# Memory values by tokens, norm weights on ScalarE, four late visits in pairs, and a shorter Newton step in a one-core decoder step

## The chip, the cores and the metric

The kernel runs on one core of a Trainium2 chip. The metric is the device time of one execution in microseconds; the comparison is between medians of several executions. A profile of one execution gives a span, from the first to the last instruction, and the rows that are quoted here.

## What is computed

One layer of a decoder for 256 prompt tokens and 8 samples of 4 new tokens each (288 columns in all), width 2048, in fp32. Cut to what matters here:

```
mkv  = (rms_norm(mem_prompt, mem_norm_g) @ w_mem_kv)     # 256 memory tokens, 4 heads of 128 keys, 4 of 128 values
h    = rms_norm(x, norm_g)
conv, q, kv6, m_q, gates = split(h @ w_in)                # 52 blocks of 128 columns
o_nsa = gated sum of attention to compressed, selected and window keys (paged cache of 2048 past tokens)
o_m   = softmax(m_q mk^T * scale) mv                      # memory attention, no mask
y     = rms_norm(x + concat(conv, silu*o_nsa, silu*o_m) @ w_out, final_g)
```

Outputs are y, the new keys and values, the window buffers, the convolution state and `mkv`.

## The kernel before

Every large product is split for accuracy: weights and activations each into a high part and a remainder, both in a reduced fp32 format (fp32r), and three products (high by high, high by low, low by high) are summed in PSUM. Weights come in halves of 128x1024 (eight 128x128 blocks). For each half `w_load` (line 221) fetches it, `w_hi` (228) makes the high part on ScalarE, `w_lo` (233) the remainder on VectorE, and `product_half` (250) runs 24 matmuls with the weight blocks as the stationary operand and the activations (256 or 288 columns) as the moving one. Half s asks ScalarE for the high part of half s+2 and VectorE for the remainder of half s+1 before its own matmuls, so the remainder of a half is made one half ahead of its use. In matmul 21 of a half the load of half s+6 is issued and one piece of x is fetched (`x_next`, 266).

Order of the program: the memory projection (eight blocks of columns, 16 halves: four blocks of keys, four of values, lines 1358 to 1361), then x's projections (queries, memory queries, keys and values, convolution, gates), then the output projection in two passes and the final norm. The memory projection gives its result as 128 features by 256 tokens. For the values, `mem_tile` (1016) multiplies each block by the tokens' norm factors (`rstd_m`) on VectorE out of PSUM into `mvt`, and `mem_rstd` (878) writes it to memory, transposes it by TensorE in pairs of 128x128 (`mvtp`) and copies it to the planes 12 to 15 of `mixed`, which hold values by tokens for the prompt's memory attention. During the same halves `prep_x` (930) makes x ready: per piece of three planes of 128x288, three VectorE operations that multiply by the norm weight of the plane and by the tokens' factors, then x's high part on ScalarE and the remainder on VectorE.

Everything that is not a large product is written as generators that are resumed at each half of a weight half (`chunk`, 161). A clock of the planner, `at`, adds up assumed costs of what was written and decides when a generator goes on; so the instruction order on each engine is fixed when the program is built, and depends on those costs.

The sampled tokens' attention is staged: tiles of 128x1024 (512 KB) of cached keys, values and windows pass through six buffers `st` (`NST`, 53) and one more that is freed when the prompt's memory queries have been used. `stages` (717) is the list of visits, sorted by a due time; `stage_stream` (746) lets a visit go ahead when its due time, its tiles and the planner's estimate of their landing allow it, `used_up` (742) gives its buffers back and `load_next` (731) issues the next loads, on SP for all but the selected values, which GpSimd gathers by page table (584). A visit is 32 or so small matmuls (fp32, 32 output rows): scores of a page group (`selk_use`, `wink_use`; tile `sk`), memory scores and values (`memk_use`, `memv_use`; `smd`, `omd`), values (`selv_use`, `winv_use`; `od`). Before its values a visit transposes the weights of the next one (`weights`, 556; tile `pv`).

The end: for the last 512 columns of y, tokens lie on partitions. `decode_rows` (1544) sums the samples' part in PSUM tile `zd`, `squares` (1551) adds the residual on VectorE and squares on ScalarE with a sum, `factors` calls `rsqrt` (199), which takes a square root on ScalarE and refines its reciprocal by one Newton step on VectorE.

## Time and profile before

| what | value |
|---|---|
| runs shown | 611.5, 613.99, 619.14 us; median 613.99 |
| the profiled execution | 616.16 us |
| its span | 614.4 us, 13419 instructions |
| mean granted TensorE clock | 0.996 |
| transfers | 190.85 MB, mean 311 GB/s |
| VectorE, ScalarE, GpSimd busy | 461.0, 285.3, 200.5 us |

How to read the rows of the profile. A row of the timeline has the start and the length in us, the engine, the line of the kernel (L120 is the helper that records every matmul, L137 the one for VectorE and ScalarE), the operation, `out<-in` by tile names, the shape, and how many were merged; in brackets stands idle time just before and what ended it. PE is TensorE's matmuls, PEld its weight loads, DVE VectorE, ACT ScalarE, POOL GpSimd, SP the queue that issues most loads. [...] An fp32 matmul leaves two records. A row of the windows view has a stretch, its length, the busy time and count of PE, PEld, DVE, ACT and POOL, the granted clock, the DMA share and GB/s.

### The profile page before, as it was taken

The page shows a single profiled execution, that of the slowest core. Times are in us where ns is not written, and L with a number is a line of the kernel's source. Part 1 is how long each engine was busy: PE and PEld are TensorE (multiplying, and loading weights), DVE is VectorE, ACT ScalarE, POOL GpSimd, SP SyncE. Part 2 cuts the span into 40 slices and gives each one's busy share as a digit, 9 for nine tenths or more (in the row PEclk, how much of TensorE's full clock was granted, in tenths as well). Part 3 has the DMA queues.
Part 4 walks back from the last instruction along what each step waited for, and adds up shares of the span by engine and source line. Part 5 has one row for each costly group of instructions (what it writes and reads, how often), then busy time and mean ns, then how long its engine had stood idle before and what let it go on. Part 6 is the DMA issues. An engine that isn't in the chain of part 4 may idle for free.

```text
span 614.4 us, 13419 instructions
## 1 busy us (share of the span) xinstructions
PE 603.0 (98%) x4919; PEld 554.0 (90%) x4919; DVE 461.0 (75%) x749; ACT 285.3 (46%) x499; POOL 200.5 (33%) x282
## 2 busy tenths in 40 slices
PE   8999999999999999999999999999999999999997
PEld 5999999989799999989889889899889989889995
DVE  4879899988485779989789888897668733357666
ACT  4755445543355444435334434543543544335552
POOL 2012544533124442433453552323111336222200
PEclk8999999999999999999999999999999999999999
DMA  8999798999968999798878898999899998859834
GB/s 285 394 403 404 258 320 300 345 310 337 365 203 280 370 407 375 250 387 298 310 232 313 284 386 273 309 318 311 289 334 332 336 353 291 288 195 411 281 130 155
DMA packets 76226, 190.85 MB, mean 311 GB/s; under 512 B 8896, under 2 KB 26464, under 8 KB 75904
## 3 DMA queue, kind: packets, MB, share of 16 engines
q0 software_dynamic: 26048, 100.48, 46.0%
q1 hardware_dynamic: 49104, 88.25, 40.4%
q10 hardware_dynamic: 1008, 1.25, 0.6%
q8 instruction: 39, 0.64, 0.4%
q14 instruction: 27, 0.22, 0.1%
HBM read 184.74 MB, written 13.60 MB: 323 GB/s over the span
## 4 chain that ended last, share of the span: by engine, by line
PE 78%; DMA 11%; DVE 8%; issue 2%; SPq 1%; ACT 0%; ACTq 0%; DVEq 0%
PE z L120 56%; DMA st<-ckc 5%; PE zr L120 4%; PE od L120 3%; DMA st<-ckk 3%; PE sk L120 3%; PE zf L120 2%; DVE wl L137 2%; DVE pooled L137 2%; PE acc L120 2%; PE s L120 2%; DMA rx<-xT 1%; DVE st L137 1%; PE pt L125 1%; DMA mraw<-memT 1%
## 5 line engine op out<-in xcount | busy, mean ns | idle before, releaser
L120 PE MATMUL z<-x,wh 128*128 128x288 f32 x1664 | 254.4, 302 | 0.0
L137 DVE TENSOR_TENSOR wl<-w,wh 128x1024 fp32r<-128x1024 f32 x147 | 185.7, 1265 | 84.6 <-PE z L120 34.9
L120 PEld LDWEIGHTS z<-x,wh 128*128 128x128 f32 x1664 | 229.7, 188 | 7.8 <-issue 6.1
L137 ACT ACTIVATE wh<-w 128x1024 fp32r<-128x1024 f32 x148 | 154.3, 1052 | 25.1 <-PE z L120 15.4
L120 PE MATMUL z<-x,wl 128*128 128x288 f32 x832 | 127.2, 295 | 0.3 <-DVE wl L137 0.3
L120 PEld LDWEIGHTS z<-x,wl 128*128 128x128 f32 x832 | 115.7, 188 | 0.8 <-DVE wl L137 0.7
L356 POOL TENSOR_TENSOR st<-st,cst 128x512 f32<-128x512 f32 x63 | 69.3, 1102 | 133.8 <-DVE st L137 49.3
L225 POOL DMA_DIRECT2D w<-w_in x104 | 58.2, 560 | 109.1 <-DVE wl L137 82.4
L137 DVE TENSOR_REDUCE pooled<-st 128x16 f32<-128x1024 f32 x63 | 76.2, 1210 | 5.8 <-POOL st L356 5.8
L137 DVE TENSOR_TENSOR st<-st,cst 128x512 f32<-128x512 f32 x63 | 43.3, 688 | 10.9 <-DMA st<-ckc 10.8
L225 POOL DMA_DIRECT2D w<-w_out x32 | 17.5, 550 | 63.0 <-DVE wl L137 43.1
L584 POOL DMA_INDIRECT st<-ckv,rows_v x26 | 27.1, 1042 | 31.9 <-PE od L120 17.4
L137 ACT ACTIVATE P<-P,nm 128x128 f32<-128x128 f32 (+1 forms) x32 | 14.2, 445 | 29.3 <-DVE nm L137 29.3
L120 PE MATMUL z<-m,wh 128*128 128x256 f32 x192 | 27.3, 287 | 0.5 <-DVE mvt L137 0.5
L120 PE MATMUL z<-y,wh 128*128 128x288 f32 x192 | 27.6, 297 | 0.0
L120 PE MATMUL z<-y1a,wh 128*128 128x288 f32 x168 | 26.7, 299 | 0.0
L120 PEld LDWEIGHTS z<-y,wh 128*128 128x128 f32 x192 | 26.3, 188 | 0.1
L120 PEld LDWEIGHTS z<-y1a,wh 128*128 128x128 f32 x168 | 23.6, 188 | 2.1 <-issue 1.2
L120 PEld LDWEIGHTS z<-m,wh 128*128 128x128 f32 x192 | 24.7, 191 | 0.8 <-issue 0.7
L120 PE MATMUL sk<-st,qz 128*32 128x256 f32 x272 | 20.4, 383 | 1.4 <-DMA st<-ckk 1.2
L120 PE MATMUL od<-st,S 128*32 128x256 f32 x256 | 18.7, 382 | 0.0
L120 PE MATMUL zf<-mixed,w 128*128 128x256 f32 x64 | 16.6, 421 | 1.9 <-DVE mixed L137 1.7
(318 smaller groups left out, 716.2 us busy)
## 6 DMA issues: line engine op xcount, KB each, us to landing
w<-w_in POOLq DMA_DIRECT2D x104, 512.0 KB
st<-ckc SPq DMA_DIRECT2D x126, 256.0 KB, 5.8
w<-w_out POOLq DMA_DIRECT2D x32, 512.0 KB
st<-ckk SPq DMA_DIRECT2D x112, 128.0 KB, 5.1
w<-w_mem SPq DMA_DIRECT2D x12, 512.0 KB, 7.1
o_wk<-wk POOLq DMA_DIRECT2D x8, 512.0 KB
o_wv<-wv POOLq DMA_DIRECT2D x8, 512.0 KB
st<-mv SPq DMA_DIRECT2D x7, 512.0 KB, 7.9
```

Source lines behind the costliest of these rows:

```text
L120: nc.tensor.matmul(out, a, b, **kw)
L125: nc.tensor.transpose(out, a, b)
L137: return getattr(self.engine, name)(*args, **kw)
L225: (nc.gpsimd if s >= ON_SYNC else nc.sync).dma_start(raws[s], wsrc[s])
L356: done.append(eng.tensor_tensor(tm[:, :, kv], tm[:, :, kv], acmp[:, kv].unsqueeze(1).unsqueeze(1).to_broadcast([128, 2, 4, 64]), op=ALU.mu ...
L584: nc.gpsimd.indirect_dma_start(t, None, ckv, bass.IndirectOffsetOnAxis(ap=rows_v[:, j * 4 + b:j * 4 + b + 1], axis=0))
```

## The change

Five edits.

1. The memory values are computed with tokens on the rows: `mem_values` replaces four calls of the block product. The stationary operand is now the split memory activations (128 tokens), the moving one the split weights, 512 columns at once; per half 12 matmuls instead of 24. The host lays these weights out accordingly (`_kpairs`). The norm factor is then one number per partition (`mr`), which ScalarE applies as it copies each of two PSUM tiles `zv` to `mixed`; the transposes and `mvt` go. The output of values is written in two pieces of 256 KB instead of four of 128 KB.
2. x's planes are multiplied by the norm weights on ScalarE as soon as they are loaded (`x_scales`, one piece per half from half 7 on); `prep_x` then multiplies a piece by the tokens' factors in one VectorE operation.
3. Four late visits are held back and run right before the next one: keys 7 with the second window's keys, memory values 0 with 1, selected values 4 with 5 and 6 with 7. For values the weights of both are transposed first. For the buffers that this takes, two more parts of the prompt's key tile `qk1` are freed once the prompt and the first group of samples are done; the samples' new keys, which lie there, are copied aside (`kn`).
4. In the final norms the Newton step has three VectorE operations after the scaled sum instead of four.
5. The samples' residual of the last columns is added by an identity matmul into `zd`, so `squares` and the final gain read PSUM directly.

```diff
+        if rest is not None:
+            act.activation(r, ssq, AF.Sqrt, scale=1.0 / D, bias=rest[0])
+            vec.scalar_tensor_tensor(v, ssq, -0.5 / D, rest[1], op0=ALU.mult, op1=ALU.add)
+            vec.reciprocal(r, r)
+            vec.scalar_tensor_tensor(t, r, r, v, op0=ALU.mult, op1=ALU.mult)
+            vec.scalar_tensor_tensor(r, t, 1.5, r, op0=ALU.add, op1=ALU.mult)
+            return
...
+    def run_half(s, mm, last, between=None):
+        m = len(mm) // 2
+        for n, (out, a, b, start, stop) in enumerate(mm):
...
+            if n == LOAD_AT * m // 12:
+                w_load(s + WR + 1)
+                next(x_next, None)
+                if s > 5:
+                    next(x_scale, None)
+            matmul(out, a, b, start=start, stop=stop)
...
+    def mem_values():
+        z = [pz.tile([128, 512], F32, name=f"zv{tt}", tag="z") for tt in range(2)]
+        def out(tt):
+            planes = mixed[:, 12 + 2 * tt:14 + 2 * tt, 0:256]
+            act.activation(planes, z[tt].rearrange("p (a n) -> p a n", a=2), AF.Copy, scale=mr[:, tt:tt + 1])
+            nc.gpsimd.dma_start(o_memv[tt].rearrange("p (a n) -> p a n", a=2), planes)
+        for h in range(8):
+            s = nhalf[0]
+            nhalf[0] += 1
+            w_hi(s + 2)
+            w_lo(s + 1)
+            wh, wl = his.pop(s), los.pop(s)
+            mm = []
+            for tt in range(2):
+                for k in range(2):
+                    hi, lo = (m_hl[n][:, 2 * h + k, tt * 128:(tt + 1) * 128] for n in range(2))
+                    w = slice(k * 512, (k + 1) * 512)
+                    early = 2 * tt + (k if h == 7 and tt else 0)
+                    mm += [(early, tt, hi, wh[:, w]), (early, tt, lo, wh[:, w]), (2.5 if h == 7 and not tt else 4, tt, hi, wl[:, w])]
+            mm.sort(key=lambda x: x[0])
...
-        if i < 4:
+        if i < 4 and ("PT", hf, i + 1) not in env:
             weights(hf, i + 1)
...
+    HELD = ((selk_use, 7), (memv_use, 0), (selv_use, 4), (selv_use, 6))
...
-            yield from u(j, tiles_of.pop((u, j)))
+            if (u, j) in HELD:
+                held.append((u, j))
+                continue
+            if u is selv_use and held:
+                for q in (j % 4 + 1, j % 4 + 2):
+                    if q < 5 and ("PT", j // 4, q) not in env:
+                        weights(j // 4, q)
+            for u, j in (*held, (u, j)) if u is not cmp_use else ((u, j),):
+                yield from u(j, tiles_of.pop((u, j)))
+                if u is not cmp_use:
+                    used_up(u, j)
...
+    def x_scales():
+        for i in range(6):
+            yield
+            k, t = xg[i]
+            for j in range(t.shape[1] // NT):
+                act.activation(xr[k + j], xr[k + j], AF.Copy, scale=C("ng")[:, k + j:k + j + 1])
...
-                for j in range(k, k + n):
-                    vec.scalar_tensor_tensor(xr[j], xr[j], g[:, j:j + 1], r, op0=ALU.mult, op1=ALU.mult)
+                xv = x.rearrange("p (k n) -> p k n", n=NT)
+                vec.tensor_tensor(xv, xv, r.unsqueeze(1).to_broadcast([128, n, NT]), op=ALU.mult)
...
+        while not env.get(("decoded", 0)):
+            yield 1
+        vec.tensor_copy(kn[1], kk[:, :, 256:NT])
+        for o in (0, 2176):
+            free.append(qk1[:, o:o + 1024])
+            load_next()
...
-    def squares(g, z):
-        vec.tensor_tensor(part[g], z, part[g], op=ALU.add)
-        act.activation(scratch[:, :part[g].shape[1]], part[g], AF.Square, accum_out=sums2[:, g:g + 1])
+    def squares(g):
+        if g < 2:
+            vec.tensor_tensor(part[g], z[g], part[g], op=ALU.add)
+        act.activation(scratch[:, :part[g].shape[1]], y_of[g], AF.Square, accum_out=sums2[:, g:g + 1])
...
+    matmul(zd[:, :128], ident, part[2], start=True, stop=False, skip_group_check=True)
     decode_rows(0, SPREAD_AT)
```

How the edits move instructions, at three places. On ScalarE in the value halves before (`wh` is a weight half's high part, `x_112` x's high part, `rx` a piece of x, `mvtp` transposed values):

```order
L137 ACTIVATE wh_558<-w_411 128x1024
L137 ACTIVATE x_112<-rx 128x864
L137 ACTIVATE wh_603<-w_455 128x1024
L137 ACTIVATE mixed<-mvtp_619 128x128 x2
L137 ACTIVATE x_112<-rx_413 128x864
L137 ACTIVATE wh_651<-w_504 128x1024
```

and now:

```order
L137 ACTIVATE rx<-rx,cst 128x288 x3
L137 ACTIVATE wh_526<-w_411 128x1024
L137 ACTIVATE x_112<-rx 128x864
L137 ACTIVATE rx_413<-rx_413,cst 128x288 x3
L137 ACTIVATE wh_557<-w_448 128x1024
L137 ACTIVATE x_112<-rx_413 128x864
```

Three scalings of 128x288 stand ahead of each weight half's high part, and a piece of x now goes from ScalarE to VectorE and back.

On VectorE in the same halves before (`wl` is a weight half's remainder, `x_113` x's remainder):

```order
L137 SCALAR_TENSOR_TENSOR rx<-rx,cst,rstd_x 128x288 x3
L137 TENSOR_TENSOR x_113<-rx,x_112 128x864
L137 TENSOR_TENSOR wl_605<-w_411,wh_558 128x1024
L137 SCALAR_TENSOR_TENSOR rx_413<-rx_413,cst,rstd_x 128x288 x3
L137 TENSOR_TENSOR mvt<-z_513,Vc 128x256
```

and now:

```order
L137 TENSOR_TENSOR rx<-rx,rstd_x 128x864
L137 TENSOR_TENSOR x_113<-rx,x_112 128x864
L137 TENSOR_TENSOR wl_559<-w_411,wh_526 128x1024
L137 TENSOR_TENSOR rx_413<-rx_413,rstd_x 128x864
L137 TENSOR_TENSOR x_113<-rx,x_112 128x864
```

One operation of 864 columns stands for three of 288, and the value tile's scaling (`mvt`) is gone.

On GpSimd's queue, near the last visits, before (gathers of selected values into `st` and `qk`, weight loads `w`):

```order
L584 DMA st_108<-ckv,rows_v 128x1024
L584 DMA st_104<-ckv,rows_v 128x1024
L584 DMA qk_793<-ckv,rows_v 128x1024
L584 DMA st_105<-ckv,rows_v 128x1024
L225 DMA w_6658<-w_out 128x1024
L225 DMA w_6690<-w_out 128x1024
L225 DMA w_6722<-w_out 128x1024
L584 DMA st_107<-ckv,rows_v 128x1024
```

and now:

```order
L629 DMA qk_665<-ckv,rows_v 128x1024
L629 DMA st_105<-ckv,rows_v 128x1024
L629 DMA st_106<-ckv,rows_v 128x1024
L629 DMA st_107<-ckv,rows_v 128x1024
L629 DMA qk_665<-ckv,rows_v 128x1024 x2
L629 DMA st_108<-ckv,rows_v 128x1024
L229 DMA w_6540<-w_out 128x1024
```

Seven gathers stand in a row where four stood, and the weight loads come behind all of them.

More of the change, by code (lines that the diff above doesn't have):

```diff
@@ L260, in product_half @@
         mm.sort(key=lambda x: x[0])
-        for n, (_, a, b) in enumerate(mm):
+        run_half(s, [(out, a, b, first and n == 0, last and n == 23) for n, (_, a, b) in enumerate(mm)], last)
+    def run_half(s, mm, last, between=None):
+        m = len(mm) // 2
+        for n, (out, a, b, start, stop) in enumerate(mm):
             if s == DIRECT and n == 0:
                 w_load(s + WR)
-            if n == LOAD_AT:
+            if n == LOAD_AT * m // 12:
                 w_load(s + WR + 1)
                 next(x_next, None)
-            matmul(out, a, b, start=(first and n == 0), stop=(last and n == 23))
-            if n == 23 and LOW_FIRST <= s < NH - 18:
+                if s > 5:
+                    next(x_scale, None)
+            matmul(out, a, b, start=start, stop=stop)
+            if n == 2 * m - 1 and LOW_FIRST <= s < NH - 18:
                 w_lo(s + 2)
-            if n % 12 == 11 and not (last and n == 23):
+            if n == 7 and between:
+                between()
+            if n == m - 1:
+                chunk()
+            if n == 2 * m - 1 and not last:
                 chunk()
@@ L305, in first_tiles @@
                     yield z[i]
+    def mem_values():
[18 more added lines that the diff above has]
+            mm.sort(key=lambda x: x[0])
+            i = [[n for n, x in enumerate(mm) if x[1] == tt] for tt in range(2)]
+            run_half(s, [(z[tt], a, b, h == 0 and n == i[tt][0], h == 7 and n == i[tt][-1]) for n, (_, tt, a, b) in enumerate(mm)],
+                     h == 7, (lambda: out(0)) if h == 7 else None)
+        assert "rstd_m" in env
+        out(1)
+        chunk()
     def proj(hi, lo, N):
@@ L771, in decode_step @@
     rstd_m = Vc
+    mr = one.tile([128, 2], F32, name="mr")
     rstd_x = zt("C", "rstd_x")
@@ L917, in token_rstd @@
         yield lag
-        r = small(3, "yr")
         w = len(groups)
@@ L930, in prep_x @@
     def prep_x():
-        g, r = C("ng"), rstd_x
+        r = rstd_x
         flat = lambda t, k, n: t[:, k:k + n, :].rearrange("p k n -> p (k n)")
@@ L1016, in mem_tile @@
     def mem_tile(i, z):
-        dst = mkT[:, i, :] if i < 4 else zt("A", "mvt")[:, :256]
-        if i < 4:
-            act.activation(dst, z, AF.Copy)
-        else:
-            yield 2
-            assert "rstd_m" in env
-            vec.tensor_tensor(dst, z, rstd_m, op=ALU.mult)
-        mem_raw[i] = dst
+        act.activation(mkT[:, i, :], z, AF.Copy)
+        mem_raw[i] = mkT[:, i, :]
+        return
+        yield
     cos, sin = C("cos"), C("sin")
@@ L1359, in decode_step @@
         then(mem_tile(i, z))
-    for i in range(2, 8):
+    for i in range(2, 4):
         then(mem_tile(i, proj(*m_hl, 256)))
+    mem_values()
     qq = xhl.tile([128, 16, 256], F32, name="qq", tag="qk0")
@@ L1530, in decode_step @@
     out = (yo[:, 0:2048], yo[:, 2048:4096], yod)
-    rest, sums2 = small(3, "yrest", 1), small(3, "ysums", 1)
+    rest, sums2 = small(6, "yrest", 1), small(3, "ysums", 1)
     quarters = small(32, "imp", 1)
@@ L1600, in decode_step @@
     rows(z[0], ws[2], 6, y, 0, False, True)
-    vec.tensor_scalar(rest, ssq[:, 0:3], 1.0 / D, EPS, op0=ALU.mult, op1=ALU.add)
-    squares(0, z[0])
+    vec.tensor_scalar(rest[:, 0:3], ssq[:, 0:3], 1.0 / D, EPS, op0=ALU.mult, op1=ALU.add)
+    vec.tensor_scalar(rest[:, 3:6], ssq[:, 0:3], -0.5 / D, -0.5 * EPS, op0=ALU.mult, op1=ALU.add)
+    squares(0)
     gains(0)
```

56 lines of the change are left out of this document (24 added, 32 removed).

## The prediction

> **What bounds the kernel now.** I read the page first: the share of each engine, and the chain that ended last.
>
> ```profile
> PE 603.0 (98%) x4919; PEld 554.0 (90%) x4919; DVE 461.0 (75%) x749; ACT 285.3 (46%) x499; POOL 200.5 (33%) x282
> PE 78%; DMA 11%; DVE 8%; issue 2%; SPq 1%; ACT 0%; ACTq 0%; DVEq 0%
> ```
>
> TensorE fills 603.0 of 614.4 us. So what the change is worth is, to first order, how much it takes out of TensorE's stream and how many waits it puts in. A mean over the span hides who paces whom, so I asked for the busy time by stage: the value projection of the memory tokens, the stretch behind it, and the late stretch in which the last visits lie.
>
> ```profile
> 35.87:60.70 24.83, 24.33 (x201) 24.03 (x200) 23.17 (x37) 14.12 (x20) 6.73 (x12) 1.00 1.03 402
> 60.70:130.00 69.30, 69.01 (x534) 67.59 (x534) 64.22 (x100) 35.45 (x62) 34.62 (x43) 1.00 0.90 305
> 310.00:541.00 231.00, 231.00 (x1985) 207.23 (x1985) 161.66 (x264) 99.33 (x185) 80.30 (x104) 1.00 0.89 311
> ```
>
> The columns are: stretch, length, busy us of PE, PEld, DVE, ACT and POOL, granted clock, DMA share, GB/s. In the first stretch VectorE is busy for 23.17 of 24.83 us, next to TensorE. From 310 to 541 us TensorE has no idle time at all and VectorE has three tenths of its time free. The first stretch is therefore paced by two engines, the last by one.
>
> **Value projection.** Before, eight halves of weights take 24 products of 256 columns each. The cost of one is its step.
>
> ```profile
> 24.15 0.28 PE L120 MATMUL z<-m,wl 128*128 128x256 f32 x1
> 24.27 0.28 PE L120 MATMUL z<-m,wh 128*128 128x256 f32 x1
> 47.91 1.60 PE L120 MATMUL z<-m,wh 128*128 128x256 f32 x12
> 49.35 0.38 PE L125 MATMUL mvtp<-cst,mvt 128*128 128x128 f32 x2
> 49.48 0.72 PE L120 MATMUL z<-m,wh 128*128 128x256 f32 x4
> 50.05 1.12 PE L120 MATMUL z<-m,wl 128*128 128x256 f32 x8
> 592.62 1.09 PE L120 MATMUL zr<-wh,y 128*128 128x512 f32 x4
> 594.01 1.09 PE L120 MATMUL zr<-wh,y 128*128 128x512 f32 x4
> ```
>
> The step at 256 columns is 0.12 us. Products of 512 columns exist in the output stage: six of them (four, and two between the quoted rows) go from 592.62 to 594.01, 0.232 us each. The new form has 96 such products for 192 old ones: 96 x 0.232 = 22.3 us for 192 x 0.12 = 23.0, 0.8 us less. The transposes of the value tiles go too: 16 products and one pair of them take 50.05 - 47.91 = 2.14 us where 16 x 0.12 is 1.92, so a pair costs 0.22. Two pairs lie in this stretch (0.45) and two behind it (0.45). The rest of the 24.83 us is 0.36 for the spread of the norm factors, which stays, and some 1.0 of waits: 24.83 - 23.04 - 0.45 - 0.36.
>
> Those waits are VectorE's.
>
> ```profile
> 49.34 1.37 DVE L137 SCALAR_TENSOR_TENSOR rx<-rx,cst,rstd_x 128x288 f32<-128x288 f32 x3
> 50.63 1.05 DVE L137 TENSOR_TENSOR x<-rx,x 128x864 fp32r<-128x864 f32 x1
> 593.33 2.35 DVE L137 TENSOR_TENSOR wl<-w,wh 128x1024 fp32r<-128x1024 f32 x2
> 54.03 0.41 DVE L137 TENSOR_TENSOR mvt<-z,Vc 128x256 f32<-128x256 f32 x1
> 54.59 1.66 PE L120 MATMUL z<-m,wh 128*128 128x256 f32 x12 [0.50 <-DVE mvt L137]
> ```
>
> Per half VectorE normalises three planes of x (1.37), splits them (1.05), splits a weight half (a step of 1.13, from two in 2.35) and, every second half, scales a value tile (0.41): 3.75 us, some 0.1 less for each operation that follows another directly, against 24 x 0.12 = 2.9 of TensorE. At 54.59 TensorE waits half a microsecond for it. In the new form the three planes are one 128x864 product of two tensors, which I price at the 1.05 of the split beside it (bounds: 0.95, the step between two such, and 1.37, as now), and the value tiles leave VectorE: 1.05 + 1.05 + 1.13, or about 3.05 when they follow each other, against 12 x 0.232 = 2.8. VectorE still loses 0.25 per half over five halves, 1.3 us. How much reserve it has:
>
> ```profile
> 36.28 1.05 ACT L137 ACTIVATE wh<-w 128x1024 fp32r<-128x1024 f32 x1
> 40.42 1.22 DVE L137 TENSOR_TENSOR wl<-w,wh 128x1024 fp32r<-128x1024 f32 x1
> 42.15 2.08 PE L120 MATMUL z<-m,wh 128*128 128x256 f32 x16
> 43.95 1.03 PEld L120 LDWEIGHTS z<-m,wl 128*128 128x128 f32 x8
> ```
>
> For the half that starts at 42.15 the low part is ready at 41.64 and wanted at 43.95: 2.3 us. That is more than 1.3, so the waits go. ScalarE takes over the 16 scalings by the norm weights.
>
> ```profile
> 592.39 0.54 ACT L137 ACTIVATE ysum<-ysum,cst 128x288 f32<-128x288 f32 x1
> 592.83 1.99 ACT L137 ACTIVATE wh<-w 128x1024 fp32r<-128x1024 f32 x2
> 50.75 0.93 ACT L137 ACTIVATE x<-rx 128x864 fp32r<-128x864 f32 x1 [1.85 <-DVE rx L137]
> ```
>
> The nearest form, a scaling of 288 columns by a column of constants, lasts 0.54, and the next operation starts 0.44 behind it. Three of them, a weight half (1.0) and x's high part (0.84 to 0.93) make 3.2 us per half, 0.4 more than TensorE's 2.8, for five halves: 2 us. The high part of the half at 42.15 ends at 37.33, 4.8 us ahead, so I take no wait from ScalarE; the bounds are 0 and, with the full 0.54 and the waits between the two engines, some 2.2. The stretch then is 22.3 + 0.36 = 22.6 us for 24.83: **2.2 us**. What hides the new work is ScalarE's 10.7 free us there; without that cover the scalings would cost 16 x 0.44 = 7 us. Behind it **0.45** for the other two pairs of transposes. The values' copies out of PSUM (two of 512 columns, for eight of 128) stay on ScalarE.
>
> **Visits in pairs.** Four visits of TensorE to staged tiles are put off and run with the next one.
>
> ```profile
> 131.00 1.22 PE L120 MATMUL z<-x,wl 128*128 128x288 f32 x8
> 132.14 1.93 PE L120 MATMUL sk<-st,qz 128*32 128x256 f32 x32
> 134.01 2.40 PE L120 MATMUL z<-x,wh 128*128 128x288 f32 x16
> 136.25 1.23 PE L120 MATMUL z<-x,wl 128*128 128x288 f32 x8
> ```
>
> From 131.00 to 136.25 are 24 products of 288 columns (24 x 0.133 = 3.19) and one visit: 2.06 us for the visit with its two changes of mode. Its own records come in eight groups of four; seven steps lie between the first and the last group, 1.93 - 0.38 = 1.55, so eight are worth 1.75. The change in and out costs 0.31, and four mergers save **1.25**. The transposes of the weights stay in number. Bounds: 0.8, if half of it stays inside a pair, and 1.25.
>
> **The tail.** The sum of the last group reads PSUM directly, and the Newton step has one operation less.
>
> ```profile
> 607.86 0.29 DVE L137 TENSOR_TENSOR ysum<-zd,ysum 128x128 f32<-128x128 f32 x1
> 608.19 0.31 ACT L137 ACTIVATE st<-ysum 128x128 f32<-128x128 f32 x1 [1.18 <-DVE ysum L137]
> 609.72 0.16 DVE L137 TENSOR_TENSOR yt<-yr 128x1 f32<-128x1 f32 x1
> 609.91 0.16 DVE L137 SCALAR_TENSOR_TENSOR yt<-yt,yv 128x1 f32<-128x1 f32 x1
> ```
>
> 0.33 from the addition's start to the square's, and 0.19 for the operation, less up to 0.2 for the identity product ahead of the last rows: **0.35** (bounds 0.2 and 0.5).
>
> **Two terms without a row of their own.** First, the order written down ahead of time shifts, since the planner's clock sees the shorter stage. One visit before meets keys that have not landed:
>
> ```profile
> 156.75 2.21 PE L120 MATMUL sk<-st,qz 128*32 128x256 f32 x22
> 160.20 1.02 PE L120 MATMUL sk<-st,qz 128*32 128x256 f32 x10 [1.24 <-DMA st<-ckk]
> ```
>
> It spans 4.5 us where the one at 132.14 spans 1.93. In the new order this visit stands one half (3.2 us) later among TensorE's halves, on a TensorE that is some 2.7 us earlier, and VectorE, which frees its buffers, is earlier too. I take 1.0 of the 2.5 us as saved (bounds 0 and 2.5). Second, a pair holds eight tiles of nine, so seven land between one pair and the next. I take 1.0 of new waits (bounds 0 and 8, below). The two cancel.
>
> Sum: 2.2 + 0.45 + 1.25 + 0.35 = **4.3 us**. The profiled execution took 616.16 us around its span of 614.4, and comes to 611.9; the median of the three runs, 613.99, is 2.2 lower and comes to **609.7**.
>
> **Rivals.** (a) ScalarE becomes the pace of the value stage. For it: 3.7 us per half with 0.54 a scaling and its waits for VectorE, since each x tile now goes ScalarE, VectorE, ScalarE, VectorE; against it the 4.8 us of reserve. Then the stage gives nothing, and 613.99 - 2.1 is **612**. [...]
>
> (b) **Slower**: the pairs wait for their tiles. Between the pair of keys and the pair of memory values, and between the last two pairs of values, seven tiles and about five weight halves of 524 KB must land, 6.3 MB. At 311 GB/s (the row of 310 to 541 us) that is 20 us, at 402 (the first stretch) 15.7; TensorE gets there 4.5 to 5 halves of 3.2 us later, and half a pair (2 us) counts too: 16.4 to 18. At the mean rate that is a wait of 2 to 4 us at each place. The gathers add to it, one per 1.3 us on GpSimd:
>
> ```profile
> 516.46 0.99 POOL L584 DMA_INDIRECT st<-ckv,rows_v x1 [4.09 <-PE od L120]
> 517.75 0.98 POOL L584 DMA_INDIRECT st<-ckv,rows_v x1 [0.30 <-issue]
> ```
>
> Seven stand in a row in the new order, 9 us, and the weight loads queue behind them. It decides from 4.3 us of waits on; 4.3 to 8 net gives 0 to 4 us more than before, **616**. Against it: the planner lets a visit in only when it holds its tiles for landed.
>
> (c) More goes than counted: the visit at 156.75 no longer waits at all, and the pairs do not wait either. Then nothing cancels, and 4.3 + 2.5 is 6.8, **607**. For it: the shift by half a microsecond that I work out for that visit is a small difference of large terms, and its loads come earlier too.
>
> **How the numbers follow.** Forecast 0.50, (a) 0.17, (b) 0.15, (c) 0.18. The range takes in (c), the forecast and (a), and leaves (b) outside: 605.5 to 614.0, with 1.5 us at either end for the spread of a median. About 2%, 12 us, is what a measurement here can tell from no change; no case reaches it, and the three runs before span 7.6 us by themselves. Faster by over 2%: 0.04; within: 0.93; slower: 0.03.
>
> **What would show it.** The value stage at 22.6 us with ScalarE under 85% and no wait of TensorE for ScalarE's high parts; if that stage is still above 24, (a). TensorE's visits of 64 records that run without a gap; if their rows carry waits for DMA, (b). The products of 512 columns in the value stage at a step of 0.23; a step well off that would make the first term wrong. The visit near 157 us without a DMA wait: (c).

## The result, and the profile after

The changed kernel took 619.47 us (median of 19 runs, 617.07 to 622.18) where the kernel before took 614.22 (19 runs): a ratio of 1.0088, 95% interval 1.0069 to 1.0107, some 5 us slower. The forecast was 609.7, with a range up to 614.0. The profiled execution took 621.35 us around a span of 619.5. The ratios here and below leave out the few executions that ran in a slower state, two of 838 and 2070 us in e6 among them.

The page of the changed kernel, engines and chain:

```profile
PE 604.8 (98%) x4817; PEld 552.1 (89%) x4817; DVE 455.9 (74%) x733; ACT 291.8 (47%) x509; POOL 201.6 (33%) x280
...
PE 86%; DMA 5%; DVE 5%; issue 2%; ACT 1%; SPq 1%; ACTq 0%; DVEq 0%
```

TensorE is busy 1.8 us longer though it has 102 products fewer. The stages of the changed kernel tell where (stretch, length, busy us of PE, PEld, DVE, ACT and POOL, granted clock, DMA share, GB/s):

```profile
36.56:59.50 22.94, 22.90 (x101) 18.23 (x101) 20.96 (x25) 19.95 (x32) 5.10 (x9) 1.00 1.03 401
310.00:480.00 170.00, 170.00 (x1454) 153.08 (x1453) 129.31 (x221) 74.53 (x144) 58.55 (x75) 1.00 0.87 308
480.00:491.00 11.00, 7.39 (x37) 7.17 (x36) 7.35 (x19) 3.07 (x6) 3.21 (x5) 0.69 1.02 408
```

The value stage is 22.94 us, near the 22.6 of the forecast. In the eleven microseconds from 480 TensorE does 37 products, and its clock is 0.69. What happened there, row by row, in time (start, length, engine, line, operation, then in brackets the idle time before it and what ended it):

```profile
475.45 0.61 PE L120 MATMUL omd<-qk 128*32 128x256 f32 x8
...
476.63 1.22 PE L120 MATMUL z<-x,wl 128*128 128x288 f32 x8
...
479.86 1.20 PE L120 MATMUL z<-x,wl 128*128 128x288 f32 x8
...
481.96 1.23 DVE L137 TENSOR_TENSOR wl<-w,wh 128x1024 fp32r<-128x1024 f32 x1 [6.30 <-issue]
482.13 0.41 ACT L137 ACTIVATE se<-z 128x288 f32<-128x288 f32 x1 [2.00 <-PE z L120]
...
483.10 0.34 DVE L137 TENSOR_SCALAR odr<-omd,cst 128x128 f32<-128x128 f32 x1
...
483.48 1.12 DVE L137 SCALAR_TENSOR_TENSOR odr<-omd,cst,odr 128x128 f32<-128x128 f32 x3
...
484.66 0.47 PE L125 MATMUL otm<-cst,odr 128*128 128x128 f32 x1 [3.60 <-DVE odr L137]
484.79 4.19 PE L120 MATMUL z<-x,wh 128*128 128x288 f32 x16
```

Read it from the end. TensorE waits 3.60 us to transpose the memory output (`otm`), and the 16 products behind it take 4.19 us, where 16 such take 2.3: half clock. It waits for VectorE's four operations that gather that output (`odr`), 483.10 to 484.60. They stand in VectorE's queue behind a weight split (`wl`), which starts at 481.96 after 6.30 us without work. The split reuses the buffer that the products at 476.63 read, and they end at 477.85. So VectorE starts 4.1 us after the last thing that it waits for is done. ScalarE's sum `se` tells the same story: it waits only for the products that end at 481.06, and starts at 482.13, 1.1 us later.

Two things could make such a start late: the signal, or the engine that waits for it. The trace decides it. Beside the rows it keeps the moment at which each engine raised its semaphore, the counter that its instructions add to and that the waiting instructions of the others name. Paired in order, for TensorE here (us):

| row ends | semaphore raised | waiting instruction starts |
|---|---|---|
| 475.63 | 476.76 | |
| 476.07 | 478.94 | |
| 476.79 | 478.99 | |
| 477.86 | 481.88 | `wl` at 481.96 |
| 481.05 | 482.10 | `se` at 482.13 |

ScalarE's rows that end at 475.79, 476.93 and 477.67 raise theirs within 0.01 us. So the waiting engines start 0.03 to 0.08 us after the semaphore is raised, and it is TensorE's semaphore that comes late, by 1.1 to 4.0 us. GpSimd works off five gathers in that stretch:

```profile
474.65 1.00 POOL L629 DMA_INDIRECT qk<-ckv,rows_v  x1 [2.74 <-PE omd L120]
...
475.96 0.97 POOL L629 DMA_INDIRECT st<-ckv,rows_v  x1 [0.30 <-issue]
...
479.74 0.95 POOL L629 DMA_INDIRECT qk<-ckv,rows_v  x1 [0.30 <-issue]
```

Five gathers, some 1.27 us apart, run from 474.65 to 480.69 us, where the signals are late. Each group of experiments below had a chip of its own, and on two of the five chips no signal of TensorE came late in any trace (0.12 us at most behind the row's end); on one of these two this kernel was run, and took 609.72 us. As each chip served one group only, the chip and the moment cannot be told apart.

### The profile page after: what moved, and what is told of

It reads as the page before. It is cut to its first block, busy times and chain, and to the rows that moved or that the text cites. A ratio compares the mean times of both kernels' runs of the same rounds, so it can differ in the third digit from the quotient of the medians.

```text
span 619.5 us, 13205 instructions
## 1 busy us (share of the span) xinstructions
PE 604.8 (98%) x4817; PEld 552.1 (89%) x4817; DVE 455.9 (74%) x733; ACT 291.8 (47%) x509; POOL 201.6 (33%) x280
## 3 DMA queue, kind: packets, MB, share of 16 engines
q10 hardware_dynamic: 1008, 1.25, 0.6%
## 4 chain that ended last, share of the span: by engine, by line
PE 86%; DMA 5%; DVE 5%; issue 2%; ACT 1%; SPq 1%; ACTq 0%; DVEq 0%
PE z L120 60%; PE zv L120 4%; PE zr L120 4%; PE od L120 3%; PE sk L120 3%; PE zf L120 3%; DMA st<-ckk 2%; PE acc L120 2%; PE s L120 2%; DMA st<-ckc 2%; DVE wl L137 1%; DVE pooled L137 1%; PE pt L125 1%; DMA mraw<-memT 1%; PE pv L125 1%
## 5 line engine op out<-in xcount | busy, mean ns | idle before, releaser
L401 POOL TENSOR_TENSOR st<-st,cst 128x512 f32<-128x512 f32 x56 | 62.2, 1111 | 105.5 <-DVE st L137 60.7
L137 DVE TENSOR_REDUCE pooled<-st 128x16 f32<-128x1024 f32 x56 | 67.8, 1211 | 7.1 <-POOL st L401 7.0
L137 DVE TENSOR_TENSOR st<-st,cst 128x512 f32<-128x512 f32 x56 | 38.2, 684 | 10.1 <-DMA st<-ckc 10.0
L137 ACT ACTIVATE se<-z 128x288 f32<-128x288 f32 x16 | 6.5, 407 | 32.3 <-PE z L120 32.3
L120 PEld LDWEIGHTS zf<-mixed,w 128*128 128x128 f32 x64 | 14.2, 225 | 5.4 <-DVE mixed L137 3.2
L120 PE MATMUL sk<-st,qz 128*32 128x256 f32 x272 | 18.2, 382 | 0.0
```

Of the source, the lines that this page charges most:

```text
L120: nc.tensor.matmul(out, a, b, **kw)
L137: return getattr(self.engine, name)(*args, **kw)
L401: done.append(eng.tensor_tensor(tm[:, :, kv], tm[:, :, kv], acmp[:, kv].unsqueeze(1).unsqueeze(1).to_broadcast([128, 2, 4, 64]), op=ALU.mu ...
```

## Experiments

The ratio is to the kernel before on the same chip, round by round, with its 95% interval, so it is not exactly the quotient of the two medians. "Late" tells whether the trace shows signals of TensorE more than 0.3 us late, "wait" is TensorE's idle time ahead of the transpose of the memory output (or at the place named), "half" the length of the stretch at half clock behind it.

| run | before | this | ratio | late | wait | half |
|---|---|---|---|---|---|---|
| the change, on record | 614.22 | 619.47 | 1.0088 (1.0069 to 1.0107) | yes | 3.60 | 6.8 |
| e4_plain_loads | 615.84 | 611.84 | 0.9926 (0.9901 to 0.9952) | 289 to 315 us only | 0 | 0 |
| e3_gathers_apart | 615.84 | 614.90 | 0.9989 (0.9956 to 1.0022) | yes | 2.21 | 3.4 |
| e5_transpose_later | 615.84 | 617.99 | 1.0039 (1.0011 to 1.0068) | yes | 0; 2.75 at `pe` | 3.4 |
| e1_no_pairs | 615.84 | 616.08 | 0.9986 (0.9959 to 1.0013) | yes | 1.48 | 0 |
| e6_before_plain_loads | 613.21 | 614.71 | 1.0007 (0.9982 to 1.0033) | no | 0 | 0 |
| e10_five_gathers | 613.21 | 609.82 | 0.9937 (0.9912 to 0.9962) | no | 0 | 0 |
| e7_one_gather_per_half | 613.21 | 615.66 | 1.0036 (1.0015 to 1.0058) | no | 0; 2.49 at `ot` | 6.8 |
| e8_pages_on_sync | 613.21 | 631.08 | 1.0285 (1.0238 to 1.0332) | no | 0; 4.19, 5.84 and 2.49 later | 6.8 three times |
| a2_change_again | 613.29 | 609.72 | 0.9948 (0.9929 to 0.9967) | no | 0 | 0 |
| e10b_five_again | 613.29 | 609.62 | 0.9948 (0.9928 to 0.9969) | no | 0 | 0 |
| e11_sums_ahead | 613.29 | 609.54 | 0.9947 (0.9931 to 0.9964) | no | 0 | 0 |
| e12_sums_ahead_apart | 613.29 | 609.50 | 0.9938 (0.9917 to 0.9958) | no | 0 | 0 |
| a3_change_third | 614.73 | 618.75 | 1.0070 (1.0043 to 1.0098) | yes | 3.25 | 6.8 |
| e11b_sums_ahead | 614.73 | 615.78 | 1.0008 (0.9979 to 1.0037) | yes | 0; 1.16 at `pe` | 0 |
| e13_split_slow | 614.73 | 614.67 | 0.9980 (0.9952 to 1.0009) | yes, but 1.3 at most at this place | 0.49 | 0 |
| e10c_five_third | 614.73 | 616.89 | 1.0026 (0.9994 to 1.0058) | yes | 3.62 | 3.4 |
| e14_split_slow_there | 616.00 | 622.30 | 1.0104 (1.0049 to 1.0159) | yes | 7.25 | 6.8 (and 3.4 near 305 us) |
| e12b_ahead_apart | 616.00 | 612.49 | 0.9954 (0.9924 to 0.9983) | yes | 0; 0.86 at `pe` | 0 (but 3.4 near 304 us) |

**First group, one chip: is it the gathers, the order, the bytes, or the pairs?** Theory A is the reading above; B holds the written order guilty, C the traffic, D the pairs as such. The change itself was not run on this chip, so its 1.0088 and 1.0070 stand beside these ratios from other chips.

e4 loads other rows plainly instead of gathering. The order on TensorE, VectorE and GpSimd stays.

```diff
 def selv_load(j, b, t):
+    if j > 3:
+        nc.gpsimd.dma_start(t, ckv[(j * 4 + b) * 128:(j * 4 + b + 1) * 128])
+        return
     nc.gpsimd.indirect_dma_start(t, None, ckv, bass.IndirectOffsetOnAxis(ap=rows_v[:, j * 4 + b:j * 4 + b + 1], axis=0))
```

> The gathers of the second group of sequences' selected values (16 tiles of 512 KB) are plain loads of other rows, same queue, same bytes, same order on every engine; so the decoded values of those sequences are not the reference's. Theory A (TensorE's completion signals come late, up to 4 us, while GpSimd works off five to seven gathers in a row, and the transpose of the memory output waits 3.6 us for it): the wait near 481 us is under 0.5 us, the second stretch of half clock is gone, and the time is 613.5 (612.5 to 615). Rival B (the written order itself: VectorE's four operations of the memory output stand behind a weight split, a chain that waits whatever the loads are): 619.5, wait still above 3 us. Rival C (the bytes: seven tiles beside the weights fill the DMA engines and everything comes late): 619.5 too, the wait within 1 us of what it was.

Measured 611.84, 0.9926. In e4's rows at the same place the transpose waits for nothing; the split follows its release, and ScalarE's sum comes 0.04 us after the products (478.94):

```profile
477.74 1.20 PE L120 MATMUL z<-x,wl 128*128 128x288 f32 x8
...
478.78 0.27 PE L125 MATMUL otm<-cst,odr 128*128 128x128 f32 x1
...
478.98 0.41 ACT L137 ACTIVATE se<-z 128x288 f32<-128x288 f32 x1 [2.48 <-PE z L120]
```

Same order, same bytes, same queue: B and C fall. That this chip does delay signals shows in the same trace, from 289 to 315 us, where gathers are left. Times the 614.22 of the record it is 609.7, below the 612.5 to 615 that was forecast.

e3 lets no more than two gathers go at a time (three at the start, since one more buffer is freed):

```diff
     def load_next():
+        gathers = 0
         while nl[0] < len(loads) and free:
             f, u, j, n = loads[nl[0]]
+            if f is selv_load and j > 3:
+                if later[0] > now[0]:
+                    return
+                gathers += 1
+                if gathers > 2:
+                    later[0] = now[0] + 2
+                    spawn(load_later(), 2)
+                    return
```

> No more than three gathers of the second group stand in a row, a weight load between each two or three; TensorE's and VectorE's order near the memory output is that of the change. Theory A: the signals are at most 1.5 us late as in the kernel before, the wait of the transpose falls from 3.6 to 1 us or less, no second stretch of half clock: 614.5 (613 to 616). Rival B: 619.5, wait still above 3 us. Rival C: 619 to 620, since the same bytes come in the same stretch.

The time is as A said (0.9989), the wait is not: 2.21 us and a stretch at half clock, where 1 us or less and none were forecast. The edit spreads little: the trace has the five at 470.86, 472.17 and 473.45, then, behind one weight load, at 475.29 and 476.56. The split still starts 2.7 us late (on record 4.1). The seven later gathers it parts into four and three, and there TensorE's semaphore is 1.4 us late at most, for 3.6 to 4.0 in the six traces with seven in a row on such a chip.

e5 puts the transpose of the memory output one half later.

```diff
     def mem_out():
...
-        yield from until(VEC)
+        yield from until(VEC, WAIT + 3.2)
```

> The planner waits 3.2 us more before it writes down the transpose of the memory output, which stands a half of weights later; the five gathers in a row stay. All theories that put the loss at this wait: the wait is under 0.5 us, no second stretch of half clock, 614.5 (613 to 616.5). If the 3.6 us wait was only in the profiled execution and the loss is elsewhere (rival D: the loss is spread over the pairs): 618 to 620.

A miss in size. The wait there is gone, but the split is late here too (it starts at 480.63), VectorE works behind it almost without a break up to the sums for the next transpose (`pe`) at 489.60, and in e5's TensorE rows the wait turns up 6 us later:

```profile
483.70 0.27 PE L125 MATMUL otm<-cst,odr 128*128 128x128 f32 x1
...
489.94 0.33 PE L125 MATMUL pe<-cst,odr 128*128 128x128 f32 x1 [2.75 <-DVE odr L137]
```

e1 takes the pairs out: no visit is held.

```diff
-    HELD = ((selk_use, 7), (memv_use, 0), (selv_use, 4), (selv_use, 6))
+    HELD = ()
```

> The change without its pairs (no visit is held back; the two more buffers stay). Theory A: single visits free four buffers at a time, the memory output sees runs of one and four gathers, so no wait there; but eight gathers now stand in a row near 500 us, and a wait of 1 to 3 us may show where something on VectorE or ScalarE is due then: 615 (613 to 618). Rival D (pairs as such cost): 613. If the loss is not in the pairs at all: 620.

615 was forecast; 0.9986 came (613.4 us for 614.22), and a wait of 1.48 us at the memory output, behind four gathers in a row, where none was expected. The time alone would fit D, which said 613. What decides against D is e4: the pairs stay, and the loss goes. The pairs make the run of gathers longer.

**Second group, another chip: what gathers cost, and remedies.** e6 is e4's edit in the kernel before. e10 is e4 with a later bound, so that the run of five is gathered and only the rows behind it are loaded plainly; e7 is e3 with one gather at a time:

```diff
-    if j > 3:
+    if j * 4 + b > 20:
...
-                if gathers > 2:
+                if gathers > 1:
```

e8 loads the values by pages, as the keys are:

```diff
+    def selv_pages(j, b, t):
+        first = 128 + j * 16 + b
+        for i, v in enumerate(page_ids(first, 4, 4)):
+            nc.sync.dma_start(t[32 * i:32 * i + 32], ckv.rearrange("(n p) c -> n p c", p=32)[ds(v, 1)].rearrange("a p c -> (a p) c"))
...
-    stages += ... some(selv_load, selv_use, 1, 4)
+    stages += ... some(selv_pages, selv_use, 1, 4)
```

> The kernel before, with the second group's 16 gathers as plain loads of other rows on the same queue (the decoded values of those sequences are not the reference's). Theory A (gathers in a row delay TensorE's signals, and only the change puts a wait within their reach): 0 to 1.5 us below the kernel before, so 613 to 614 where that is 614.2, and the change with plain loads stays 3 to 4.5 us below this one. Rival E (plain loads are simply cheaper, by bytes or issue, whatever the change): this kernel gains as much as the change did, 7 to 9 us, to 606.

> The change with plain loads for 11 of the second group's 16 tiles (values not the reference's there); only the run of five gathers that follows the pair of memory values stays. Theory A: the wait of the transpose of the memory output is back at 3 to 4 us, with one or two stretches of 3.4 us at half clock behind it; time 615 to 617.5 where all plain gave 609.7 on the same scale (before 614.2). Rival F (the seven in a row near 520 us and the other gathers carry the loss): 610 to 611, wait under 1 us.

> Each of the second group's gathers has a weight load, a half of weights (3.2 us), between it and the next. Theory A with a delay that builds up over gathers in a row: signals less than 0.7 us late, no wait of the transpose over 1 us, full clock: 610.5 to 612.5 where before is 614.2, unless tiles of the pairs now land late (then a DMA wait of 1 to 3 us ahead of the last pairs, 613). Rival G (each gather delays by itself, however far the next is): a wait of 2 us or more stays, 614 to 616.

> The second group's selected values come by pages as its keys do: four loads of 128 KB a tile on SyncE's queue, with page numbers read from the table, no gather on GpSimd. Theory A: no late signal behind 470 us, no wait of the transpose, full clock: 609.7 to 611.5 where before is 614.2. Rival C (the bytes beside the weights): 615 or more. A risk that both share: SyncE needs 3 us to issue a tile, so the seven tiles of a pair take 21 us and TensorE may wait 1 to 4 us for the last of them: then 611 to 614.

e6 gains nothing (1.0007): on this chip there was no late signal to lose, not even beside the gathers that e6 keeps. e10 contradicts A as I had it: five gathers in a row, and 609.82 with no wait. But no trace of this group shows a late signal, not even beside the gathers near 290 us, where all four of the first group do. It was another chip, and the question became whether the gathers delay signals at all, or only there. e7 and e8 lose for reasons of their own, mostly in the output stage behind the last visits. In e7 the last gather ends at 530.5 us (518.3 in a2), so late that the output of the last values (`od`) is summed when VectorE has other work; in e8 SyncE issues pages until 538.7 us, the residual's load goes out behind them, and VectorE waits for it with the weight splits behind. In e8 a pair also waits 4.19 us for a tile, as its expectation feared. First e7's TensorE rows in that stage, then e8's rows there and at that pair:

```profile
545.06 0.63 PE L120 MATMUL zr<-wl,y1a 128*128 128x512 f32 x2
...
548.18 0.30 PE L125 MATMUL ot<-cst,odr 128*128 128x128 f32 x1 [2.49 <-DVE odr L137]
```

```profile
516.91 0.61 PE L120 MATMUL od<-st,S 128*32 128x256 f32 x1 [4.19 <-DMA st<-ckv]
...
553.38 1.06 DVE L137 TENSOR_TENSOR ysum<-ysum,xr 128x864 f32<-128x864 f32 x1 [8.77 <-DMA xr<-xT]
...
555.63 1.22 PE L120 MATMUL zr<-wl,y1a 128*128 128x512 f32 x2 [5.84 <-DVE wl L137]
```

The 5.84 us of TensorE in e8 come from the 8.77 of VectorE; the 2.49 of e7 are a wait for the sums of the last values' output.

**Third group: the change itself, and a better order.** e11 emits the four sums directly after the pair, ahead of the weight split, and leaves the transpose where it was; e12 adds e3's spreading.

```diff
-            spawn(mem_out(), 1)
+            g = mem_out()
+            spawn(g, next(g))
...
-        yield from until(VEC)
+        yield from until(VEC, WAIT + 3.2)
```

> The changed kernel once more, to see it beside the others on one chip. In the four runs just before (on another chip than the first four) no signal of TensorE came late, the five gathers in a row included; on the first chip they came late in every kernel with gathers. Theory H (the late signals belong to gathers on some chips or in some conditions, not to gathers as such): if this execution shows late signals, the wait at the memory output is 3 to 4 us and the time 5 us above the kernel before; if it shows none, the wait is under 0.5 us and the time 4 us below the kernel before (ratio 0.993). Rival I (the run of seven gathers and the others after the five are what makes the signals late): late signals and 5 us above before here, and 4 us below before in the run with five gathers alone.

> The run with five gathers alone (11 of the second group's tiles by plain loads) once more. Theory H: goes with the run of the change beside it: both with late signals (wait 3 to 4 us, 1 to 3 us above before) or both without (4 us below before). Rival I: 4 us below before whatever the change does.

> The change with VectorE's four operations of the memory output one place ahead: in front of the weight split that they stood behind; TensorE's order is the same, gathers as in the change. Where signals come late by up to 4 us: the operations end about 480.6, the transpose waits under 0.5 us, the time is 6 us below the change (ratio to before 0.998 to 1.000, the seven gathers still cost 0.7 to 1.5 us). Where none come late: the same as the change, within 0.5 us.

> Both: VectorE's operations of the memory output ahead of the weight split, and no more than three gathers in a row. Where signals come late: 1 to 2 us below the kernel with the operations ahead alone, ratio to before 0.995. Where none come late: within 1 us of the change, 0.993 to 0.995.

All four at 609.5 to 609.7, no late signal. The unchanged change ran 10 us faster than on record. The rows of a2 that answer to those of the record:

```profile
472.40 1.22 PE L120 MATMUL z<-x,wl 128*128 128x288 f32 x8
...
473.72 1.22 DVE L137 TENSOR_TENSOR wl<-w,wh 128x1024 fp32r<-128x1024 f32 x1 [2.29 <-ACT S L137]
...
475.24 1.12 DVE L137 SCALAR_TENSOR_TENSOR odr<-omd,cst,odr 128x128 f32<-128x128 f32 x3
...
475.62 1.20 PE L120 MATMUL z<-x,wl 128*128 128x288 f32 x8
...
476.66 0.27 PE L125 MATMUL otm<-cst,odr 128*128 128x128 f32 x1
...
476.86 0.41 ACT L137 ACTIVATE se<-z 128x288 f32<-128x288 f32 x1 [2.48 <-PE z L120]
```

The split starts 0.1 us after its release (473.62), the sums end at 476.36, and the transpose comes at 476.66: **0.3 us in hand**. Any signal later than that is a wait of TensorE.

**Fourth and fifth group: what stayed open.** e13 and e14 repeat one weight split three times, e13 four halves too early by a wrong count, e14 at the place meant:

```diff
             (eng or vec).tensor_tensor(los[s], raws[s], his[s].bitcast(F32), op=ALU.subtract)
+            for _ in range(3 if s == 118 else 0):
+                nc.vector.tensor_tensor(los[s], raws[s], his[s].bitcast(F32), op=ALU.subtract)
```

> The changed kernel a third time, beside the others of this call. Theory H (its time follows whether TensorE's signals come late while gathers are worked off, and that belongs to the chip or its condition): one of two cases and nothing between. Late signals in its trace: wait at the memory output 3 to 4 us, ratio to before 1.005 to 1.011. None late: no wait over 0.5 us there, ratio 0.993 to 0.996.

> VectorE's four operations of the memory output in front of the weight split, once more. With late signals in the trace: no wait over 0.7 us at the memory output, 5 to 6 us below the change beside it. Without: within 0.5 us of the change.

> The change with one weight split, the one ahead of the memory output's operations on VectorE, done four times instead of once (3.4 us more on VectorE at that one place; the result is the same). It puts by hand, where no signal is late, the delay that the late signal brought. Theory H: VectorE has 0.3 us in hand there, so TensorE waits 3.0 to 3.4 us at the transpose, and a stretch of 3.4 or 6.8 us at half clock follows: 4.7 to 6.8 us above the change. Rival J (a single wait is made up later, and the loss on record was made of many small delays): under 1.5 us above the change. Where signals are late as well, the two delays add to 5 to 7 us of wait.

> Gathers kept only in the run of five behind the pair of memory values (the other 11 tiles of the second group by plain loads, so values there are not the reference's). With late signals in the trace of the change beside it: here too, wait 3 to 4 us, 4 to 7 us above what all plain loads gave (theory H); under 1 us of wait if the gathers behind these five make the signals late (rival I). Without late signals: as the change, within 0.5 us.

This chip showed late signals again, and the change took 1.0070. e10c settles what e10 could not: with the five gathers alone in the second group the wait is 3.62 us, and signals are late nowhere behind them, so it is the gathers, on such a chip, and rival I falls. Its rows at the place:

```profile
478.65 0.94 POOL L632 DMA_INDIRECT qk<-ckv,rows_v  x1 [0.30 <-issue]
478.77 1.20 PE L120 MATMUL z<-x,wl 128*128 128x288 f32 x8
...
483.59 0.47 PE L125 MATMUL otm<-cst,odr 128*128 128x128 f32 x1 [3.62 <-DVE odr L137]
```

e11b takes the wait away, but is 3 us below the change and not 5 to 6; 1.16 us reappear ahead of `pe` and a little where splits come late. e13 is a miss, since its delay stood in the wrong place and VectorE had it in hand but for 0.5 us. The gathers of its run start at 474.54, 475.85 and then 478.08, signals come 1.3 us late at most there, and it is 4 us below the change; that the added splits caused this is not shown.

> The weight split directly ahead of the memory output's operations on VectorE done four times instead of once (3.4 us more on VectorE, result the same); the run before it had the repeats four halves too early. Theory H on a chip without late signals: VectorE has 0.3 us in hand, so TensorE waits 3.0 to 3.4 us at the transpose, one or two stretches of 3.4 us at half clock follow, and the time is 4.7 to 6.8 us above the change on such a chip: ratio to before 1.002 to 1.006. Rival J (a single wait is made up later): 0.995 to 0.997. On a chip with late signals the delays add: wait of 5 to 7 us, ratio 1.010 to 1.016.

> VectorE's operations of the memory output ahead of the weight split, and no more than three gathers in a row, once more. On a chip with late signals: no wait over 1 us at the memory output, none at the last pairs, ratio to before 0.996 to 1.000, below the kernel with the operations ahead alone (1.0008 there). On a chip without: 0.993 to 0.996, as before.

e14 adds 3.75 us of VectorE's work to a late signal, and TensorE waits 7.25, just above the forecast 5 to 7. The ratio is 1.0104, as forecast, but its interval overlaps that of the change (1.0070, 1.0088 on other chips): that a longer wait at this place is not made up later is likely and not shown (on a chip without late signals it was not tried). The rows of e12b, both remedies on a chip with late signals:

```profile
473.74 0.61 PE L120 MATMUL omd<-qk 128*32 128x256 f32 x8
...
474.92 1.22 PE L120 MATMUL z<-x,wl 128*128 128x288 f32 x8
...
476.53 0.35 DVE L137 TENSOR_SCALAR odr<-omd,cst 128x128 f32<-128x128 f32 x1 [2.58 <-PE z L120]
...
478.80 1.22 DVE L137 TENSOR_TENSOR wl<-w,wh 128x1024 fp32r<-128x1024 f32 x1 [0.76 <-remote]
...
479.19 0.27 PE L125 MATMUL otm<-cst,odr 128*128 128x128 f32 x1
```

The pair ends at 474.35 and the sums start at 476.53, 2.2 us late; the products at 474.92 end at 476.14 and the split starts at 478.80, 2.7 us late. Both signals are late, and the transpose waits for neither: the sums stand ahead of the split and have 1.1 us in hand in spite of it (they end at 478.04). The time is 612.49, ratio 0.9954 (0.9924 to 0.9983); without late signals it was 609.50, 0.9938 (0.9917 to 0.9958). **This version beats the kernel before on both kinds of chip**, by some half a per cent, in one run on each; it beats the change where signals come late (1.0070 to 1.0088 there), and stands level with it where they do not (0.9948).

## Why the prediction was wrong, point by point

The forecast of 609.7 is what the change does where signals come in time (a2: 609.72, ratio 0.9948, which is 3.2 us, interval 2.0 to 4.4, against the 4.3 of the sum). That the two times agree to the tenth is luck: the gain was 1.1 us smaller, and the kernel before took 613.29 there and not 613.99. On record the change took 10 us more. Each term, by a2's trace where nothing else is said:

**Value stage: right, 1.9 us for 2.2.** It takes 22.94 us in a2 and in the record's trace alike, for a forecast of 22.6:

```profile
35.61:58.55 22.94, 22.90 (x101) 18.23 (x101) 20.96 (x25) 19.93 (x32) 5.08 (x9) 1.00 1.03 401
```

In the record's trace the products of 512 columns run at 2.72 us for twelve, a step of 0.227 (0.232 was taken). TensorE is idle for 0.04 us, so the reserve paid for VectorE as said, and rival (a) falls, though ScalarE reached 19.93 us, 87%, where I had drawn the line at 85. Three scalings by the norm weights take 1.38 us on ScalarE in the record's trace (from 38.98 us), as long as VectorE's three operations took before (1.37); the stage gained, since VectorE was the engine that was full (23.17 us of 24.83 before, 20.96 of 22.94 now). What I did not count is behind the stage: VectorE has used up its lead there, and its next halves give some 0.8 us of the 2.65 forecast (2.2 and the 0.45 of the other transposes) back (by before's half at 83.41 us, a2 is 1.8 ahead).

**The waiting visit: better than taken.** It has no wait any more and spans what an undisturbed one does: 2.5 us and not 1.0, by the trace of before on record. Rival (c) had this part right. But in e6, where the kernel before is the same up to there, this visit spans 3.1 us (156.22 to 159.36) and not 4.4, so on that chip there were only 1.3 us to save.

**Pairs: each merger right, the sum too large.** 24 products and the pair of memory values take from 466.48 to 473.46, 6.98 us; less 3.19 that is 3.79 for two visits, where two single ones took 2 x 2.06: 0.33 saved, 0.31 forecast. But two small visits that rode along with a key visit now stand alone, and the last pair waits for ScalarE's copy of its weights, so I put the four at about 0.5 and not 1.25. No pair waits for a DMA in any trace but e8's, whose tiles come another way: rival (b) came nearest in sign and size (616), with a mechanism that did not happen. The rows of a2 for this and the point before:

```profile
158.57 1.93 PE L120 MATMUL sk<-st,qz 128*32 128x256 f32 x32
...
528.91 0.40 PE L120 MATMUL od<-st,S 128*32 128x256 f32 x1 [0.53 <-ACT S L137]
```

**Tail: right**, 0.4 for 0.35 (14.15 to 13.74 us).

**New waits: the step that failed.** "I take 1.0 of new waits (bounds 0 and 8, below)", with seven tiles between the pairs as the reason. In a2 there is one of 0.41 us near 241 us, besides the 0.53 of the last pair; on record one wait and the half clock behind it cost 6.4 us (below). I looked for them at tiles and DMAs. The wait that came is none of these: VectorE's sums of the memory output moved behind a weight split, and that left 0.3 us in hand before TensorE wants them. Before, they end at 482.29, ahead of the next split and 2.0 us before the transpose:

```profile
481.17 1.12 DVE L137 SCALAR_TENSOR_TENSOR odr<-omd,cst,odr 128x128 f32<-128x128 f32 x3
...
483.05 1.23 DVE L137 TENSOR_TENSOR wl<-w,wh 128x1024 fp32r<-128x1024 f32 x1 [0.75 <-PE z L120]
...
484.25 0.27 PE L125 MATMUL otm<-cst,odr 128*128 128x128 f32 x1
```

The order of both programs is fixed ahead of time, so the move could be seen; I priced the visits on TensorE and did not ask what each moved instruction on VectorE now stands behind. On record this place costs 3.60 us of waiting. Behind it stand 16 products in 4.19 us for 2.3, and 8 in 1.92 for 1.06 (488.77 to 490.69), some 2.8 us more: 6.4 us together. Of the rest of the 11.4 us between the spans of the record (619.5) and of a2 (608.1), 1.4 is a wait at `imp` near 217 us, 1.0 a longer one at `pt` (1.5 for 0.5), 1.0 a later start; the other 1.6 us or so are not attributed (a wait of 0.51 among late signals at 529 us is set off by the 0.53 of a2's last pair).

And the sum took for granted that a signal arrives when its row ends. The trace of before showed that it need not, in rows that the prediction did not use:

```profile
498.95 1.22 PE L120 MATMUL z<-y1a,wl 128*128 128x288 f32 x8
499.61 0.94 POOL L584 DMA_INDIRECT qk<-ckv,rows_v  x1 [0.30 <-issue]
...
501.65 0.41 ACT L137 ACTIVATE ysum<-z 128x288 f32<-128x288 f32 x1 [4.64 <-PE z L120]
501.71 1.23 DVE L137 TENSOR_TENSOR wl<-w,wh 128x1024 fp32r<-128x1024 f32 x1 [4.92 <-PE z L120]
```

The products end at 500.17. ScalarE's sum needs only them and starts at 501.65, 1.48 us late, at the end of four gathers in a row (495.79 to 500.55). There it was harmless: the remainder made at 501.71 is ready at 502.93, and the products that want it start at 507.86, 4.9 us later. Rows that end an idle time with the name of a product which ended 1.5 us before are the sign to look for; the pairs then put a fifth gather into such a run and a transpose with 0.3 us of reserve behind it. What the runs show of this: with other rows of the same size loaded plainly it goes (e4), with only the five gathers left it stays (e10c), and on a chip without late signals it never comes (a2, e10b). What of a gather does it (the work on GpSimd, the scattered rows or something else) no run tells apart.

## What to carry to other kernels

When an edit moves instructions, work out for each moved one on a side engine what it now stands behind, and how much time is left before the bounding engine wants it; an engine with a quarter of its time free can still be late at one place (VectorE, busy for 74% of the span on record, held TensorE for 3.60 us). Put what the bounding engine waits for ahead of unrelated work in the queue (e12: the four sums ahead of the weight split), and do not let gathers pile up beside it (e3: seven parted into four and three delayed signals by 1.4 us instead of 3.6 to 4.0; five parted by one weight load still by 2.7). Every wait of TensorE from 2.21 us on cost more than itself here, since 3.4 or 6.8 us at half clock came with it.

## What the runs showed of the hardware

**Signals that arrive late.** Usually another engine starts 0.04 to 0.2 us after the recorded end of the products that it waits for (a2: split 473.72 after 473.62). During runs of gathers on GpSimd it is 1 to 4.2 us (a3: split 478.88 after 474.73), in the traces of the record and on three of five chips; with plain loads of the same bytes on the same queue it is not (e4), and on the other two chips not with gathers either. The kernel before took 614.2 to 616.0 us on the former and 613.2 to 613.3 on the latter. The semaphore times in the traces, paired with the rows in order, show whose signal it is: TensorE's come up to 5.0 us behind the row's end (4.0 on record, 5.0 in e11b), in the same traces ScalarE's at most 0.01 us and VectorE's at most 0.03; in the eight traces of the two other chips TensorE's come 0.12 us behind at most. So the end of a row is not the signal: on record `wl` starts 4.1 us after the row's end (477.86) and 0.08 us after the semaphore (481.88). Whether the results reach PSUM late or only the signal is sent late, no row shows.

One more trace of the same trouble: in the twelve traces with late signals 11 to 27 of about 1565 semaphore updates of TensorE, ScalarE and VectorE are not recorded at all, each within 2 us after a gather's start; in the eight others none is missing. So updates near gathers are lost to the recording too in these traces, and whether recording has a part in the delay is open: every run here has a recorded span and clock. Why chips differ stays open: nothing here could vary it.

**Half clock behind a wait.** In the record's trace the granted clock is half for 6.83 us, from 483.91 to 490.73; the wait of 3.60 us begins at 481.06, so the stretch begins 2.85 us into it. A part of it:

```profile
485.00:490.00 5.00, 5.00 (x23) 5.00 (x23) 4.46 (x11) 2.47 (x4) 0.86 (x1) 0.50 1.06 429
```

By run: waits up to 1.48 us left no such stretch, a wait of 1.51 at `pt` near 303 us did in two traces (e12b, e14) and not in nine others, one of 1.69 in e6 did not, and every wait from 2.21 us on did: 2.21, 2.75 and 3.62 gave 3.4 us of half clock, 2.49 (with 1.27 more behind 0.3 us of work), 3.25, 3.60, 4.19, 5.84 and 7.25 gave 6.8. So a wait of 2.21 us was enough here, one of 1.69 was not, and the stretches come in two lengths, 3.4 and 6.8 us. What sets the length, and why 1.51 us brought a stretch in two traces of eleven, no run shows.
